# A root-mean-square pooling kernel: the small first piece on partitions 32 to 91 instead of 0 to 29

## The chip, the cores and the metric

One core of one Trainium2 chip, the chip otherwise idle. The metric is the device time of one execution in microseconds (us); lower is better. Beside it stands the *span* of a profiled or timed execution, from the first to the last counted instruction.

## The reference

```python
x = randn(32, 256, 4096) float32;  p = 2.0;  kernel_size = 4
for i in range(4096 // 4):
    window = abs(x[:, :, 4*i:4*i+4]) ** p
    result[:, :, i] = mean(window, axis=-1) ** (1.0 / p)
```

Each output is the root of the mean of four squares. 134.22 MB go in and 33.55 MB go out.

## The kernel before

The input is taken as one flat array. 22 big loads, most of them 128 rows of 13,184 columns (52,736 bytes a row), rotate through three input buffers. ScalarE (ACT) squares a load in place, VectorE (DVE) sums groups of four into an output buffer, ACT takes the root, and a store sends two loads' worth of results out. Loads are issued from the SP queue, the first seven big stores from the ACT queue, the last four from the SP queue.

The total does not divide evenly into such loads. 840 columns times 128 elements, 430 KB (420.0 KB in the views, which count in units of 1024), remain. This *small piece* is loaded first of all, into a corner of an output buffer that is still free:

```python
    Q = 30
    odd = ODD * P // Q                       # 840 * 128 / 30 = 3584
    t = o_tiles[1][0:Q, 0:odd]
    nc.sync.dma_start(out=t, in_=xf[(total - ODD) * P:total * P].rearrange("(p w) -> p w", p=Q))
    ahead = 0
    while ahead < n and loads[ahead][0] < X_SLOTS:
        load(ahead)                          # the first three big loads, same queue
        ahead += 1
    nc.vector.tensor_tensor(out=t, in0=t, in1=t, op=mybir.AluOpType.mult)
    ...                                      # sum of four, root, store of 30 x 896
```

and a big store is issued as soon as its root is taken:

```python
    def root(g, o, ends):
        r = nc.scalar.activation(out=o, in_=o, func=Act.Sqrt, scale=1.0 / k)
        ...
        if ends and g not in late:
            store(g, nc.scalar)
```

Of the kernel before, what the change touches and what calls it, by code (L numbers as in the profile page):

```python
# [1 line left out]

# [4 lines left out]


@with_exitstack
def kernel(  # L10
    ctx: ExitStack,
    tc: tile.TileContext,
    x: bass.AP,
    p: float,
    kernel_size: int,
    out: bass.AP,
):








    nc = tc.nc

    assert float(p) == 2.0, "kernel specialized for p == 2"
    k = int(kernel_size)
    assert k == 4, "kernel specialized for kernel_size == 4"  # L30

    P = nc.NUM_PARTITIONS
    fp32 = mybir.dt.float32
    Act = mybir.ActivationFunctionType
    xf = x.rearrange("b c l -> (b c l)")
    of = out.rearrange("b c l -> (b c l)")
    total = xf.shape[0] // P

    W, O_W = 13184, 6592
    X_SLOTS, O_SLOTS = 3, 2  # L40
    slots = [[(W, [W])]] * 17 + [[(W, [6592, 6592])]]
    slots += [[(6592, [6592]), (6592, [6592])], [(6592, [6592]), (4216, [2112, 2104])]]
    ODD = 840
    groups = [2] * 9 + [3, 1]
    late = {7, 8, 9, 10}
    in_x = {9: (2, 0), 10: (2, 4944)}
    FINE, ENDS, LAG = {21}, {19, 20}, 1
    PAIRS = 15


    loads = [(s, sum(w for w, _ in slot[:j]), *slot[j]) for s, slot in enumerate(slots)
             for j in range(len(slot))]
    n = len(loads)
    assert sum(w for _, _, w, _ in loads) + ODD == total

    firsts = [sum(groups[:g]) for g in range(len(groups))]
    assert sum(groups) == n
    group_of = [g for g, count in enumerate(groups) for _ in range(count)]
    columns = [sum(w for _, _, w, _ in loads[firsts[g]:firsts[g] + groups[g]])
               for g in range(len(groups))]  # L60

    x_pool = ctx.enter_context(tc.tile_pool(name="x_pool", bufs=1))
    o_pool = ctx.enter_context(tc.tile_pool(name="o_pool", bufs=1))

    x_tiles = [x_pool.tile([P, W], fp32, name=f"xt{j}") for j in range(X_SLOTS)]
    o_tiles = [o_pool.tile([P, O_W], fp32, name=f"ot{j}") for j in range(O_SLOTS)]
    ctx.enter_context(tc.manual_schedule())

    def block(flat, g, div):
        at, width = sum(columns[:g]) * P // div, columns[g] * P // div  # L70
        return flat[at:at + width].rearrange("(p w) -> p w", p=P)

    xs = {}
    by_load = []

    def load(i):
        s, at, w, _ = loads[i]
        v = x_tiles[s % X_SLOTS][:, at:at + w]
        g = group_of[i]
        src = sum(loads[j][2] for j in range(firsts[g], i))  # L80
        nc.sync.dma_start(out=v, in_=block(xf, g, 1)[:, src:src + w])  # L81
        xs[i] = v

    ots = {}




    stores = {}
    by_act = []  # L90
    sums = []

    def follows(ins, before):
        for b in before:
            tc.declare_no_dep(ins.ins, b.ins, reason="follows from other waits")

    def store(g, queue):
        stores[g] = queue.dma_start(out=block(of, g, k), in_=ots[g])  # L98

    def root(g, o, ends):  # L100
        r = nc.scalar.activation(out=o, in_=o, func=Act.Sqrt, scale=1.0 / k)  # L101
        follows(r, by_act[:-1] + list(stores.values()))
        by_act.append(r)
        if ends and g not in late:
            store(g, nc.scalar)

    def total_sum(o, v, i):
        add = mybir.AluOpType.add
        if i < PAIRS:
            r = nc.vector.tensor_reduce(  # L110
                out=o, in_=v.rearrange("p (n j) -> p n j", j=k),
                axis=mybir.AxisListType.X, op=add,
            )
            follows(r, sums[:-1])
            sums.append(r)
            return

        q = v.rearrange("p (n j) -> p n j", j=k)
        front = v[:, 0:v.shape[1] // 2]
        h = front.rearrange("p (n j) -> p n j", j=2)  # L120
        r = nc.vector.tensor_tensor(out=h, in0=q[:, :, 0:2], in1=q[:, :, 2:4], op=add)  # L121
        follows(r, sums[:-1] + by_load)
        r = nc.vector.tensor_tensor(out=o, in0=h[:, :, 0], in1=h[:, :, 1], op=add)  # L123
        follows(r, sums[:-1])
        sums.append(r)


    Q = 30
    odd = ODD * P // Q
    t = o_tiles[1][0:Q, 0:odd]  # L130
    nc.sync.dma_start(out=t, in_=xf[(total - ODD) * P:total * P].rearrange("(p w) -> p w", p=Q))  # L131
    ahead = 0
    while ahead < n and loads[ahead][0] < X_SLOTS:
        load(ahead)
        ahead += 1
    nc.vector.tensor_tensor(out=t, in0=t, in1=t, op=mybir.AluOpType.mult)  # L136
    o = o_tiles[1][0:Q, odd:odd + odd // k]
    nc.vector.tensor_reduce(  # L138
        out=o, in_=t.rearrange("p (n j) -> p n j", j=k),
        axis=mybir.AxisListType.X, op=mybir.AluOpType.add,  # L140
    )
    nc.scalar.activation(out=o, in_=o, func=Act.Sqrt, scale=1.0 / k)  # L142
    stores["odd"] = nc.scalar.dma_start(
        out=of[(total - ODD) * P // k:total * P // k].rearrange("(p w) -> p w", p=Q), in_=o,
    )
    pending = []
    done = 0
    for i in range(n):
        s, _, w, chunks = loads[i]
        while ahead < n and loads[ahead][0] < s + X_SLOTS:  # L150
            load(ahead)
            ahead += 1
        g = group_of[i]
        if i == firsts[g]:
            t, first = (o_tiles[g % O_SLOTS], 0) if g not in in_x else (x_tiles[in_x[g][0]], in_x[g][1])
            ots[g] = t[:, first:first + columns[g] // k]
            summed = rooted = 0
        assert sum(chunks) == w
        c = 0
        for step in chunks:  # L160
            v = xs[i][:, c:c + step]
            r = nc.scalar.activation(out=v, in_=v, func=Act.Square)  # L162
            follows(r, by_act[:-1])
            by_act.append(r)
            total_sum(ots[g][:, summed:summed + step // k], v, i)
            while pending and pending[0][0] <= done - LAG:
                root(*pending.pop(0)[1:])
            done += 1
            c += step
            summed += step // k  # L170
            ends = summed == columns[g] // k
            if ends or i in FINE or (i in ENDS and c == w):
                pending.append((done - 1, g, ots[g][:, rooted:summed], ends))
                rooted = summed
    for job in pending:
        root(*job[1:])
    for g in sorted(late):
        store(g, nc.sync)


# [1 line left out]
_INS = ['x', 'p', 'kernel_size']  # L182
_OUTS = [((32, 256, 1024), 'float32')]

_NUMBERS = {'p': 2.0, 'kernel_size': 4}


# [26 lines left out]
```

## Time and profile before

| | before |
|---|---|
| time, median of the first 3 runs | 394.47 us (394.25 to 395.67) |
| span of the profiled run | 392.4 us |
| DVE busy, ACT busy | 68%, 71% |
| share of the 16 DMA engines' time that the two queues take | 99.3% |
| small piece: issue to landing | 4.3 us |
| first big square starts at | 20.66 us |

How to read it: compute engines have time to spare and the DMA engines have none, so look at what those do and at what they do *not* do in each stretch. A transfer is split over the DMA engines: in the records, 16 completion writes follow each big load and 15 the small one. From 24 to 340 us exactly 16 packets are under way for 97% of the time, and 99% of them start within 4 ns of the end of another. I read this as each engine working through its own row of packets one after the other, so a packet that takes longer than its bytes warrant is lost time for that engine. I call this the **loss**: the sum of (time of a packet minus the usual time of its size) over all packets of a stretch, divided by 16.

### The profile page before, as it was taken

What the parts mean: (1) busy time and instruction counts of PE and PEld (TensorE: products, weight loads), DVE (VectorE), ACT (ScalarE), POOL (GpSimd) and SP (SyncE); (2) the same over time, 40 slices, a digit from 0 to 9 for tenths busy, and PEclk for the clock granted to TensorE, in tenths of its full rate; (3) what the DMA queues carried; (4) which work ended last, traced back from release to release, by engine and by line L of the source; (5) the groups of instructions that cost most, each with busy time, mean ns of one, the idle gap of its engine ahead of it and who ended that gap; (6) DMA issues with size and microseconds to landing.
All of it is one profiled execution on the core that took longest, in us unless ns stands there. A gap on an engine that the chain in (4) does not pass through costs nothing.

```text
span 392.4 us, 183 instructions
## 1 busy us (share of the span) xinstructions
DVE 268.5 (68%) x35; ACT 280.2 (71%) x39; POOL 0.2 (0%) x4
## 2 busy tenths in 40 slices
DVE  4307898885769476948693769396928690989481
ACT  1085879919990899099909990998099919999991
POOL 0000000000000000000000000000000000000000
DMA  8999999999999998999999999999999999999997
GB/s 318 425 441 430 446 441 441 411 435 470 430 398 430 473 430 387 430 473 430 411 441 438 430 473 425 392 430 430 430 435 452 446 430 446 409 430 416 446 430 321
DMA packets 4842, 167.77 MB, mean 428 GB/s; under 512 B 558, under 2 KB 558, under 8 KB 716
## 3 DMA queue, kind: packets, MB, share of 16 engines
q1 hardware_dynamic: 3789, 144.04, 85.3%
q10 hardware_dynamic: 1053, 23.73, 14.0%
HBM read 134.22 MB, written 33.55 MB: 428 GB/s over the span
## 4 chain that ended last, share of the span: by engine, by line
DMA 47%; ACT 34%; DVE 16%; SPq 0%; ACTq 0%; issue 0%
DMA xt<-in_x_dram 47%; ACT xt L162 28%; DVE ot L110 14%; ACT ot L101 6%; DVE xt L121 1%; DVE xt L123 1%; ACT xt L101 1%; ACTq L98 0%; SPq L81 0%; SPq L131 0%
## 5 line engine op out<-in xcount | busy, mean ns | idle before, releaser
L162 ACT ACTIVATE xt<-xt 128x13184 f32<-128x13184 f32 (+3 forms) x24 | 222.2, 9272 | 91.4 <-DMA xt<-in_x_dram 89.8
L110 DVE TENSOR_REDUCE ot<-xt 128x3296 f32<-128x13184 f32 x15 | 208.3, 13886 | 88.6 <-ACT xt L162 88.6
L101 ACT ACTIVATE ot<-ot 128x6592 f32<-128x6592 f32 x9 | 51.1, 5681 | 0.0
L121 DVE TENSOR_TENSOR xt<-xt 128x3296 f32<-128x3296 f32 (+3 forms) x9 | 34.5, 3836 | 22.5 <-ACT xt L162 22.2
L123 DVE TENSOR_TENSOR ot<-xt 128x3296 f32<-128x3296 f32 (+1 forms) x4 | 10.9, 2734 | 0.1
L142 ACT ACTIVATE ot<-ot 30x896 f32<-30x896 f32 x1 | 0.9, 948 | 10.9 <-DVE ot L138 10.9
L101 ACT ACTIVATE xt<-xt 128x3296 f32<-128x3296 f32 (+3 forms) x4 | 5.8, 1449 | 2.3 <-DVE xt L123 2.3
L136 DVE TENSOR_TENSOR ot<-ot 30x3584 f32<-30x3584 f32 x1 | 3.9, 3879 | 5.1 <-DMA ot<-in_x_dram 5.1
L123 DVE TENSOR_TENSOR xt<-xt 128x1648 f32<-128x1648 f32 (+2 forms) x5 | 7.0, 1407 | 0.2
L138 DVE TENSOR_REDUCE ot<-ot 30x896 f32<-30x3584 f32 x1 | 3.9, 3874 | 0.0
L142 ACT ACT_TABLE_LOAD x1 | 1.3, 1283 | 0.7 <-PEq L195 0.7
L195 POOL MEMSET const-bfloat16-1.0<- 128x1 bf16 x1 | 0.1, 101 | 0.0
L195 POOL MEMSET const-uint8-127<- 128x1 uint8 x1 | 0.1, 101 | 0.0
L195 POOL MEMSET const-float32-0.0<- 128x1 f32 x1 | 0.1, 98 | 0.2 <-issue 0.2
L195 POOL MEMSET const-float32-1.0<- 128x1 f32 x1 | 0.1, 98 | 0.0
## 6 DMA issues: line engine op xcount, KB each, us to landing
xt<-in_x_dram SPq DMA_DIRECT2D x18, 6592.0 KB, 31.3
out_dram<-ot ACTq DMA_DIRECT2D x7, 3296.0 KB, 27.0
xt<-in_x_dram SPq DMA_DIRECT2D x3, 3296.0 KB, 24.2
out_dram<-ot SPq DMA_DIRECT2D x2, 3296.0 KB, 26.2
out_dram<-xt SPq DMA_DIRECT2D x1, 2472.0 KB, 9.2
xt<-in_x_dram SPq DMA_DIRECT2D x1, 2108.0 KB, 23.7
out_dram<-xt SPq DMA_DIRECT2D x1, 527.0 KB, 5.9
ot<-in_x_dram SPq DMA_DIRECT2D x1, 420.0 KB, 4.3
```

Source lines behind the costliest of these rows:

```text
L101: r = nc.scalar.activation(out=o, in_=o, func=Act.Sqrt, scale=1.0 / k)
L110: r = nc.vector.tensor_reduce(out=o, in_=v.rearrange("p (n j) -> p n j", j=k), axis=mybir.AxisListType.X, op=add,)
L121: r = nc.vector.tensor_tensor(out=h, in0=q[:, :, 0:2], in1=q[:, :, 2:4], op=add)
L123: r = nc.vector.tensor_tensor(out=o, in0=h[:, :, 0], in1=h[:, :, 1], op=add)
L136: nc.vector.tensor_tensor(out=t, in0=t, in1=t, op=mybir.AluOpType.mult)
L138: nc.vector.tensor_reduce(out=o, in_=t.rearrange("p (n j) -> p n j", j=k), axis=mybir.AxisListType.X, op=mybir.AluOpType.add,)
L142: nc.scalar.activation(out=o, in_=o, func=Act.Sqrt, scale=1.0 / k)
L162: r = nc.scalar.activation(out=v, in_=v, func=Act.Square)
L195: nc = _bacc.Bacc("TRN2", target_bir_lowering=False, num_devices=1)
```

## The change

The intent: with 30 rows on partitions 0 to 29, two to each of 15 DMA engines (30 packets, 15 completion writes), the second packets take 741 to 1092 ns where their bytes are worth 529. With 60 half rows on partitions 32 to 91, four to each of the 15 engines, I expected each packet to take the time of its bytes alone, about 265 ns. The arithmetic is split at partition 64 into two sets of instructions.

```diff
-    Q = 30
+    LOW, Q = 32, 60
     odd = ODD * P // Q
-    t = o_tiles[1][0:Q, 0:odd]
-    nc.sync.dma_start(out=t, in_=xf[(total - ODD) * P:total * P].rearrange("(p w) -> p w", p=Q))
+    wide = o_tiles[1]
+    nc.sync.dma_start(
+        out=wide[LOW:LOW + Q, 0:odd],
+        in_=xf[(total - ODD) * P:total * P].rearrange("(p w) -> p w", p=Q),
+    )
 ...
-    nc.vector.tensor_tensor(out=t, in0=t, in1=t, op=mybir.AluOpType.mult)
-    o = o_tiles[1][0:Q, odd:odd + odd // k]
-    nc.vector.tensor_reduce(...)
-    nc.scalar.activation(out=o, in_=o, func=Act.Sqrt, scale=1.0 / k)
+    for a, b in ((LOW, 64), (64, LOW + Q)):
+        t, o = wide[a:b, 0:odd], wide[a:b, odd:odd + odd // k]
+        nc.vector.tensor_tensor(out=t, in0=t, in1=t, op=mybir.AluOpType.mult)
+        nc.vector.tensor_reduce(...)
+        nc.scalar.activation(out=o, in_=o, func=Act.Sqrt, scale=1.0 / k)
 ...                     # the small store takes its rows from the same partitions
```

More of the change, by code (lines that the diff above doesn't have):

```diff
@@ L135 @@
         ahead += 1
-    nc.vector.tensor_tensor(out=t, in0=t, in1=t, op=mybir.AluOpType.mult)
-    o = o_tiles[1][0:Q, odd:odd + odd // k]
-    nc.vector.tensor_reduce(
-        out=o, in_=t.rearrange("p (n j) -> p n j", j=k),
-        axis=mybir.AxisListType.X, op=mybir.AluOpType.add,
-    )
-    nc.scalar.activation(out=o, in_=o, func=Act.Sqrt, scale=1.0 / k)
+    for a, b in ((LOW, 64), (64, LOW + Q)):
+        t, o = wide[a:b, 0:odd], wide[a:b, odd:odd + odd // k]
+        nc.vector.tensor_tensor(out=t, in0=t, in1=t, op=mybir.AluOpType.mult)
+        nc.vector.tensor_reduce(
+            out=o, in_=t.rearrange("p (n j) -> p n j", j=k),
+            axis=mybir.AxisListType.X, op=mybir.AluOpType.add,
+        )
+        nc.scalar.activation(out=o, in_=o, func=Act.Sqrt, scale=1.0 / k)
     stores["odd"] = nc.scalar.dma_start(
-        out=of[(total - ODD) * P // k:total * P // k].rearrange("(p w) -> p w", p=Q), in_=o,
+        out=of[(total - ODD) * P // k:total * P // k].rearrange("(p w) -> p w", p=Q),
+        in_=wide[LOW:LOW + Q, odd:odd + odd // k],
     )
```

## The prediction

> **What bounds the kernel now.** I read the page first (shares of the engines, the DMA row, the queues), then the busy time by stages, then the timeline of the start, and last the single packet records of the trace.
>
> From the page:
>
> ```profile
> span 392.4 us, 183 instructions
> ...
> DVE 268.5 (68%) x35; ACT 280.2 (71%) x39; POOL 0.2 (0%) x4
> ...
> DMA  8999999999999998999999999999999999999997
> ...
> q1 hardware_dynamic: 3789, 144.04, 85.3%
> q10 hardware_dynamic: 1053, 23.73, 14.0%
> HBM read 134.22 MB, written 33.55 MB: 428 GB/s over the span
> ```
>
> The two compute engines idle for about 30% each. The 16 DMA engines are busy in every one of the 40 slices, and the two queues together take 85.3 + 14.0 = 99.3% of them. The stages (us, then DVE, ACT, POOL busy, PE clock, DMA share, GB/s) say the same:
>
> ```profile
> 0.00:8.00 8.00, 2.90 (x1) 1.28 (x1) 0.20 (x4) 1.00 0.89 324
> ...
> 24.00:80.00 56.00, 41.66 (x3) 46.81 (x5) 0.00 (x0) 1.00 1.00 430
> 80.00:340.00 260.00, 183.30 (x15) 184.75 (x21) 0.00 (x0) 1.00 1.00 432
> 340.00:384.00 44.00, 34.82 (x15) 42.46 (x11) 0.00 (x0) 1.00 1.00 432
> ```
>
> From 24 to 384 us the DMA share is 1.00. Only the first 8 us and the tail are below. The kernel is bound by transfers from end to end. The chain that ended last names ACT and DVE for half of the span, but that is only the route by which buffers come free: the queue behind them never ran dry.
>
> A budget: a 52,736-byte packet, half of a 13,184-column row, takes 1947 ns in the median, 27.09 GB/s for one engine, 433.4 GB/s for 16. 167.77 MB at that rate are 387.1 us. The first packet starts at 1.74 us and the last ends at 390.99. So only 390.99 - 1.74 - 387.1 = 2.15 us of engine time is lost in the whole kernel. That is all that any rearrangement of transfers could win.
>
> The start, from the timeline:
>
> ```profile
> 0.73 0.45 SPq L131 DMA_DIRECT2D ot<-in_x_dram  x1
> 1.24 1.30 SPq L81 DMA_DIRECT2D xt<-in_x_dram  x3
> 5.09 3.88 DVE L136 TENSOR_TENSOR ot<-ot 30x3584 f32<-30x3584 f32 x1 [5.09 <-DMA ot<-in_x_dram]
> 9.01 3.87 DVE L138 TENSOR_REDUCE ot<-ot 30x896 f32<-30x3584 f32 x1
> 12.92 0.95 ACT L142 ACTIVATE ot<-ot 30x896 f32<-30x896 f32 x1 [10.90 <-DVE ot L138]
> 13.89 0.64 ACTq L143 DMA_DIRECT2D out_dram<-ot  x1
> 20.66 11.19 ACT L162 ACTIVATE xt<-xt 128x13184 f32<-128x13184 f32 x1 [6.79 <-DMA xt<-in_x_dram]
> ```
>
> The small piece is the first transfer in the queue; the big loads stand right behind it. Its own arithmetic (5.09 to 13.87 us) is over nearly 7 us before the first big load lands at 20.66, so nothing waits for that. Its transfer, however, stands in front of all others on the engines.
>
> The packet records (us from the span's start) of it and of the first big load:
>
> ```
> 14,336-byte packets: 30; first of each engine starts 1.73 to 2.21, takes 542 to 965 ns
>                          second of each engine takes 741 to 1092 ns; last ends 3.98
> first 52,736-byte packets: 16; start 3.03 to 3.98, take 2245 to 2908 ns, end 5.52 to 6.25
> all later ones: 1947 ns median
> last completion write of each engine: 390.32 to 391.00
> ```
>
> At 27.09 GB/s a packet of 14,336 bytes should take 529 ns; the last ones of the small piece take 1085, twice that.
>
> [...]
>
> **The change part by part.**
>
> Bytes: none added. Still 28,672 per engine for 15 engines.
>
> The load. [...] A 3584-byte packet takes 140 ns where its bytes are worth 132, so a packet costs about 8 ns besides, and two more per engine 0.02 us. [...]
>
> What the engines lost before: the 30 packets took 25.34 us together where 30 x 529 ns are 15.89, so 9.45; the 16 first big packets took 39.18 where 16 x 1.949 are 31.18, so 8.00. (9.45 + 8.00) / 16 = 1.09 us per engine. [...] The earliest of the first big packets, starting at 3.03 ahead of any completion write, belongs to the engine that has no share of the small piece[...]; it still took 2473 ns, 0.53 too many. The very last, which began when the small piece was done, had 0.30 too many. I therefore take 0.3 to 0.5 us as start-up of a first big transfer that stays.
>
> The slowest engine sets the end, and its lag is never made up: 391.00 - 6.25 = 384.75 for the latest and 390.32 - 5.52 = 384.80 for the earliest, if lags keep their order. So the quantity to predict is when the slowest engine ends its first big packet, now 6.25. After: start at the latest 2.2, plus 1.08 for four packets, plus some 0.2 for the first packet's latency (my choice), makes 3.5; plus 1.95 + 0.1 to 0.5 for the first big packet makes 5.5 to 6.0. Saved 0.25 to 0.75; with no start-up loss at all, 1.0. I choose **0.65 us**.
>
> Compute. DVE: (3879 - 146) ns are 3584 columns at one per 1.04 ns, so a half instruction is about 1.87 + 0.15 = 2.02 us, four of them 8.1 instead of 7.75. ACT: 13,184 columns take 11.19 us, 0.849 ns each, so 896 columns are 0.76 and the rest of 948 ns is 0.19; two of 448 columns are 2 x 0.57 = 1.14. In all half a microsecond more, off the path: done near 13.5 us, against 20 for the first load. The order of instructions shows two more on DVE, one on ACT, and nothing else moved. Path cost: 0.
>
> The store. 30 packets of 3584 bytes at 140 ns become 60 of 1792 at some 74: per engine 0.28 to 0.30 us, +0.02. It alternates with 1.95 us packets of the loads, so with four per engine it lands some 4 us later; nobody waits for it.
>
> Sum: -0.65 + 0.02 + 0 = about -0.6; 394.47 becomes **393.8 us**, 0.2% less.
>
> **Rivals.**
> (a) The full microsecond: [...]the big packets begin at 3.0 everywhere. For it: the doubled second packets. Against: the free engine's 2473 ns. Time 393.4.
> (b) Nothing: [...] The first packets spread over 0.48 us for 15 engines, 32 ns per engine; if that is per descriptor, 16 ns each, 30 more cost 0.48 us and the start moves from 3.0 to 3.5 on the last engine, which eats most of the gain. Time 394.2 to 394.5. Against: 3.5 is still earlier than 3.98.
> (c) The gain is absorbed: the lag of the slowest engine is not what ends the kernel but the last stores behind ACT. Against: from 340 to 384 us the share is 1.00, so data were still queued when ACT was done. Time 394.4.
> (d) Slower: twice as many, half as long rows in the small store disturb the first loads. At 74 ns each I see at most 0.1 us.
>
> **Range and chances.** (a) and (b) bracket the change at -1.1 and 0. The three runs of before spread from 394.25 to 395.67, so the median itself moves by some tenths. Range 393.1 to 394.7. A 2% change would be 7.9 us, over three times all the engine time lost in the kernel[...]: faster 0.01, within 2% 0.98, slower 0.01.
>
> **What would show it.** Right: the small piece's packets take about 265 ns each, none above 400 after the first of each engine; its load lands about 0.5 us earlier than 4.3 us after issue; the first multiply starts near 4.5 rather than 5.09; the first big square at about 20.0 rather than 20.66; the span is 0.4 to 1.0 shorter with the DMA share still 1.00 in the middle. Wrong: packets of 530 ns for 7168 bytes[...], first big packets starting later than 3.5 (descriptors, rival b), or an earlier first square with an unchanged end (rival c).

Some passages are cut; the cuts are marked. In the paragraph on the load, the terms 2.12 us before and 1.06 after are cut; with the 0.02 for two more packets per engine, which stays, they came to about 1.04 us saved. The sum of -0.65, +0.02 and 0 is about -0.6 us, hence 393.8. Its 0.65 is an estimate from the time at which the slowest engine's first big row ends; that the 60 packets would take the time of their bytes at the measured 27.09 GB/s was my assumption. So was, in rival (b), that 60 rows instead of 30 delay the rows behind them; a *descriptor*, there and in the expectation of e5, stands for one row of a transfer.

## More of the kernel before

All runs quoted here are in the fast state, with a granted clock of 1.00.

Below, *light start* stands for a small piece on partitions 32 to 91, 32 to 95 or 0 to 127, *heavy start* for one on 0 to 29, 0 to 31, 0 to 59, 0 to 63 or 64 to 95.

## The result, and the profile after

The changed kernel took 395.12 us in the median (394.91 to 396.56, 6 runs). The kernel before, taken up to 6 runs on the same chip, stood at 395.54 (394.25 to 395.85). The ratio of the fast runs is 1.0005, with a 95% interval of 0.9983 to 1.0026: no difference. Ratios here are the mean time of one kernel's fast runs over that of the other's fast runs of the same rounds, so they are not quite the ratios of the medians.

The page of the changed kernel answers the page of before line by line:

```profile
span 393.6 us, 186 instructions
...
DVE 268.7 (68%) x37; ACT 280.5 (71%) x40; POOL 0.2 (0%) x4
...
DMA  9999999999999999999999999999999999999997
...
q1 hardware_dynamic: 3819, 144.04, 85.2%
q10 hardware_dynamic: 1083, 23.73, 14.0%
HBM read 134.22 MB, written 33.55 MB: 426 GB/s over the span
```

The bytes are the same, the packets are 60 more. The first digit of the DMA row went from 8 to 9, yet the rate over the span went from 428 to 426. The stages (same columns as in the prediction: us, DVE, ACT, POOL busy, PE clock, DMA share, GB/s) show where:

```profile
0.00:8.00 8.00, 3.88 (x2) 1.28 (x1) 0.20 (x4) 1.00 0.92 370
...
24.00:80.00 56.00, 41.94 (x4) 46.33 (x5) 0.00 (x0) 1.00 1.00 426
80.00:340.00 260.00, 181.94 (x15) 184.00 (x20) 0.00 (x0) 1.00 1.00 432
340.00:384.00 44.00, 34.84 (x14) 42.45 (x12) 0.00 (x0) 1.00 1.00 431
```

The first 8 us move more (370 GB/s, before 324). The stretch from 24 to 80 us moves less (426, before 430), with the engines just as busy: packets there took longer. The start of the timeline:

```profile
0.73 0.45 SPq L132 DMA_DIRECT2D ot<-in_x_dram  x1
1.24 1.30 SPq L81 DMA_DIRECT2D xt<-in_x_dram  x3
4.08 2.02 DVE L142 TENSOR_TENSOR ot<-ot 32x1792 f32<-32x1792 f32 x1 [4.08 <-DMA ot<-in_x_dram]
6.13 2.01 DVE L143 TENSOR_REDUCE ot<-ot 32x448 f32<-32x1792 f32 x1
...
12.27 0.57 ACT L147 ACTIVATE ot<-ot 28x448 f32<-28x448 f32 x1 [3.52 <-DVE ot L143]
12.87 0.64 ACTq L148 DMA_DIRECT2D out_dram<-ot  x1
19.99 11.19 ACT L168 ACTIVATE xt<-xt 128x13184 f32<-128x13184 f32 x1 [7.14 <-DMA xt<-in_x_dram]
```

The small piece is there a microsecond earlier (first multiply at 4.08 instead of 5.09), and the first big square starts at 19.99 instead of 20.66, 0.67 us earlier. So the gain is real. Now the third and the fifth big square, with the first big store between them, in the timeline of before:

```profile
51.77 11.19 ACT L162 ACTIVATE xt<-xt 128x13184 f32<-128x13184 f32 x1 [4.39 <-DMA xt<-in_x_dram]
68.58 0.37 ACTq L98 DMA_DIRECT2D out_dram<-ot  x1
...
88.87 11.19 ACT L162 ACTIVATE xt<-xt 128x13184 f32<-128x13184 f32 x1 [8.68 <-DMA xt<-in_x_dram]
```

and of the changed kernel:

```profile
51.27 11.19 ACT L168 ACTIVATE xt<-xt 128x13184 f32<-128x13184 f32 x1 [4.38 <-DMA xt<-in_x_dram]
68.08 0.37 ACTq L98 DMA_DIRECT2D out_dram<-ot  x1
...
89.25 11.19 ACT L168 ACTIVATE xt<-xt 128x13184 f32<-128x13184 f32 x1 [9.56 <-DMA xt<-in_x_dram]
```

Both squares wait for their load. At the third the changed kernel leads by 0.50 us; at the fifth it trails by 0.38. In between, with the first big store, 0.88 us were lost: 37.10 us from one square to the other before, 37.98 after.

The single packet records, in us from the span's start, say the same for the DMA engines themselves (median and last of the 16 engines' completion writes; loads numbered from 1, and load 18 is the last of full width):

```
                                     before            changed
first big row of an engine ends      5.52 to 6.25      5.18 to 5.67
loss up to 10 us                     1.12              0.51
load 4 complete, median / last       66.68 / 66.91     66.23 / 66.51
loss from 1 us before to 9 us after
  the first big store's issue        0.15              1.11
load 5 complete, median / last       88.17 / 88.49     88.58 / 88.87
load 18 complete, median / last      339.33 / 339.85   340.05 / 341.00
last write of all                    391.00            392.18
```

Two more differences are read off the run lists. The time minus the span is 1.78 us for the kernel before (mean of 44 later runs) and 2.11 to 2.17 for the changed kernel: about **0.36 us lie outside the span**. And the kernel before has times at two levels, near 394.1 and near 395.6: of the 44 later runs, spans lie between 392.2 and 394.2, 24 of them at or above 393.0. I call these the lower and the upper level. The first three runs, from which I predicted, had 394.47, 395.67 and 394.25.

### The profile page after: what moved, and what is told of

Same layout as the page of the kernel before. It is cut to its first block, busy times and chain, and to the rows that moved or that the text cites. A ratio compares the mean times of both kernels' runs of the same rounds, so it can differ in the third digit from the quotient of the medians.

```text
span 393.6 us, 186 instructions
## 1 busy us (share of the span) xinstructions
DVE 268.7 (68%) x37; ACT 280.5 (71%) x40; POOL 0.2 (0%) x4
## 4 chain that ended last, share of the span: by engine, by line
DMA 48%; ACT 34%; DVE 16%; SPq 0%; ACTq 0%; issue 0%
DMA xt<-in_x_dram 48%; ACT xt L168 28%; DVE ot L110 14%; ACT ot L101 6%; DVE xt L121 1%; DVE xt L123 1%; ACT xt L101 1%; ACTq L98 0%; SPq L81 0%; SPq L132 0%
## 5 line engine op out<-in xcount | busy, mean ns | idle before, releaser
L147 ACT ACTIVATE ot<-ot 32x448 f32<-32x448 f32 (+1 forms) x2 | 1.1, 574 | 9.7 <-DVE ot L143 9.7
L142 DVE TENSOR_TENSOR ot<-ot 32x1792 f32<-32x1792 f32 (+1 forms) x2 | 4.0, 2016 | 4.1 <-DMA ot<-in_x_dram 4.1
L143 DVE TENSOR_REDUCE ot<-ot 32x448 f32<-32x1792 f32 (+1 forms) x2 | 4.0, 2010 | 0.1
```

Of the source, the lines that this page charges most:

```text
L143: nc.vector.tensor_reduce(out=o, in_=t.rearrange("p (n j) -> p n j", j=k), axis=mybir.AxisListType.X, op=mybir.AluOpType.add,)
```

## The experiments

Four jobs of four kernels, five rounds each, on the same chip within a job, each timed against the kernel before. All 16 gave correct results. Each loss quoted is read from one profiled execution of its kernel.

### e1: the kernel before again (a control)

No edit.

> The kernel before, unchanged, against itself: a control. Ratio 1.000; the width of its interval is what five rounds can tell. Theory A (the stall of 1.10 us per engine at 70 us in the profile after is chance): this profile too can show stalls of 0.1 to 1 us per engine, at other or the same places, and their sum differs from the 0.28 us per engine that the first profile of before showed beyond the start. Theory B (the change makes that stall, by bringing the engines into step): the excess beyond the start stays near 0.3 us per engine. In both the start loses 1.1 us per engine, the first big packets end at 5.5 to 6.3 us.

Measured: 394.14 us, ratio 0.9994 (0.9975 to 1.0012). Start loss 1.11, loss at the first big store 0.42. One of six runs was at the upper level. So five rounds tell apart about 0.2%, and the loss at the store is not nothing in the kernel before, but under half of the changed kernel's.

### e2: the changed kernel again

No edit.

> The changed kernel again. Both theories: the start as seen, first big packets end at 5.2 to 5.7 us. Theory A: no stall near 1 us per engine at 70 us, or one elsewhere; ratio to before 0.9985 (0.6 us less), from 0.997 to 1.000. Theory B: again a stall of about 1 us per engine at 69 to 75 us, ratio 1.000 to 1.003.

Measured: 395.44 us, ratio 1.0020 (0.9998 to 1.0042). Start loss 0.51, as in the first profile. Loss at the first big store 0.88, again at 69 to 74 us. Chance (theory A) wanted it gone; theory B had it right. Load 4 is complete at 66.17 in the median (e1: 66.57), load 5 at 88.33 (e1: 88.34): a lead of 0.40 us before the store, none after it.

### e3 and e4: three more small loads each

```diff
 # e3: on the kernel before; e4: on the changed kernel, rows LOW:LOW + Q
+    for j in range(3):
+        nc.sync.dma_start(out=x_tiles[2][0:Q, j * odd:(j + 1) * odd], in_=<the small piece>)
```

> The kernel before with the load of the small piece made three times more, into columns of the third input buffer that its first big load overwrites (30 rows on partitions 0 to 29; the copies are read by nobody, the result stays right). Bytes alone: three times 28,672 per engine at 27.09 GB/s, 3.2 us. If [...], three times 2.12 = 6.4 us longer than before, ratio 1.016. If [...]: 3.2 us, ratio 1.008.

> The changed kernel with its small load made three times more, in the same way (60 rows on partitions 32 to 91). Both: four packets of 272 ns per engine and load, three times 1.09 = 3.3 us longer than the changed kernel, ratio to before 1.007. If what is gained at the start reaches the end (the theory of the prediction), this kernel is 3.1 + 0.6 = 3.7 us faster than the one with three more loads of 30 rows; if it is given back on the way, the two differ by under 1 us.

(Conditions of e3: the added loads take twice the time of an engine's bytes, as the doubled packets suggest, or just that time.)

Measured: e3 400.77 us, ratio 1.0156 (1.0135 to 1.0177); e4 398.88 us, ratio 1.0111 (1.0090 to 1.0132), four runs each. Against e1 and e2 of the same rounds, three more loads cost 400.77 - 394.14 = 6.63 us with 30 rows, **2.21 us each**, and 398.88 - 395.44 = 3.44 us with 60 rows on partitions 32 to 91, **1.15 each**. The estimates were 2.12 (twice 28,672 bytes at 27.09 GB/s) and 1.09 (four packets of 272 ns). The medians of e1 and e2 depend on how many runs fell on which level, so these slopes are rough; the engines' median completion of load 4, which comes before that, gives 2.26 ((73.34 - 66.57) / 3) and 1.24 ((69.88 - 66.17) / 3). So a load on partitions 0 to 29 costs nearly twice the time of one on 32 to 91, and this does reach the end of the kernel: it would make about 1.06 us for the one load of the real kernels. But e3 and e4 differ by only 1.89 us, which is neither the 3.7 nor the "under 1 us" of the expectation: beside the part that grows with the number of loads there is a fixed amount that the layout on partitions 32 to 91 pays. With no load added it is 1.30 us slower in these rounds (395.44 - 394.14) though its small load is 1.06 us quicker, so the fixed amount is about 2.4 us here, a part of it the levels.

### e5: 60 rows, but on partitions 0 to 59

```diff
-    LOW, Q = 32, 60
+    LOW, Q = 0, 60
-    for a, b in ((LOW, 64), (64, LOW + Q)):
+    for a, b in ((LOW, LOW + Q),):
```

> The changed kernel with its 60 rows on partitions 0 to 59, arithmetic in one piece again (two DVE instructions, one ACT)[...]. If [...]: second half of the packets near 540 ns for 7168 bytes, start loss 1.0 to 1.1 us per engine, first big packets end at 5.6 to 6.3 us; if the number of descriptors made the difference, the start is like the changed kernel's (0.48 us lost). Time minus span: 1.8 us if the 0.3 us that the changed kernel has outside its span go with its split arithmetic, 2.1 if with the 60 rows.

(Condition: the start's loss goes with the partitions.)

Measured: 395.31 us, ratio 1.0013 (0.9997 to 1.0029). Start loss 1.05, first big rows end at 5.49 to 6.16: as in the kernel before. So it is the partitions, not the finer cut, that make the start heavy or light. Loss at the first big store 0.12. Time minus span 1.74 to 1.83: the extra outside the span is gone with the split arithmetic, although the rows are 60. The time itself is no better than the changed kernel's: five of the six runs are at the upper level, and in the profiled one a single engine ends 1.17 us after the last but one.

### e6: 64 rows on partitions 32 to 95

```diff
-    LOW, Q = 32, 60
+    LOW, Q = 32, 64
```

> The changed kernel with 64 rows on partitions 32 to 95: [...]. Start as in the changed kernel or 0.1 us better[...]. If the stall at the first big store comes from the engines being in step, it is as large as in the changed kernel or larger (0.9 to 1.2 us per engine), and the time 395.0 to 395.6; if it is chance, it can be absent, and the time is then 393.5 to 394.

Measured: 395.49 us, ratio 1.0024 (1.0005 to 1.0042). Start loss 0.52, loss at the first big store 1.09. With 64 rows the loss is as large as with 60 (1.11).

### e7 and e9: the first big store held back

```diff
 # e7 (failed) and e9, before the store:
+        if ends and g == 0:
+            nc.scalar.activation(out=o_tiles[1][:, 3296:6592], in_=o_tiles[0][:, 0:3296], func=Act.Square)   # e7
+            nc.scalar.activation(out=o_tiles[0][:, 0:3296], in_=o_tiles[0][:, 0:3296], func=Act.Copy)        # e9
```

> The changed kernel with one more ACT instruction (some 2.8 us, its result is overwritten) before the first big store is issued, so that this goes out at 71 instead of 68.1 us. If the stall at 70 to 74 us belongs to the issue of that store, it moves by about 3 us, to 73 to 77; if it belongs to what the loads read just then, it stays at 70 us. If only this coincidence of times makes it, it is gone and the time drops to about 393.7.

e7 did not do what I meant. Its store reads nothing that the added instruction writes, so it was issued at 68.18 us beside it. As one more sample of the changed kernel it is of use: 395.56 us, ratio 1.0020 (1.0002 to 1.0039), loss 1.04, same place. In e9 the store must wait:

> The changed kernel with the first big store really held back (the earlier attempt did not: the store did not wait for the added instruction). The added ACT instruction now copies half of that store's data onto itself, 2.9 us, so the store is issued at about 71 us. Theory S (the loss of about 1 us per engine at 70 to 74 us belongs to the store's issue): it moves to 73 to 77 us. Theory L (it belongs to what the loads read at that moment): it stays at 70 to 72.5 us. Theory C (a coincidence of the two): under 0.3 us per engine, and the lowest times go down to 393.8.

Measured: 395.35 us, ratio 1.0005 (0.9985 to 1.0025). Timeline of e9, same columns as above:

```profile
51.26 11.19 ACT L172 ACTIVATE xt<-xt 128x13184 f32<-128x13184 f32 x1 [4.38 <-DMA xt<-in_x_dram]
71.05 0.37 ACTq L98 DMA_DIRECT2D out_dram<-ot  x1
...
87.28 11.19 ACT L172 ACTIVATE xt<-xt 128x13184 f32<-128x13184 f32 x1 [4.63 <-DMA xt<-in_x_dram]
```

The store went out at 71.05, 2.97 us later than in the changed kernel, and the main group of lengthened packets starts at 73.56 to 74.2 us in place of 69.8 to 70.5. The loss is 0.69. (The fifth square comes earlier with fewer store rows in between: 72 had started when load 5 was complete, 100 in the changed kernel.) So **the loss belongs to the store**, not to what the loads read at 70 us. Both e7 and e9 have one ACT instruction more and a time minus span of 1.74 to 1.83 us, like the kernel before.

### e8: the kernel before with the arithmetic in halves

```diff
+    for h in range(2):          # two halves of the columns, 30 partitions each
+        th, oh = ...
         nc.vector.tensor_tensor(...); nc.vector.tensor_reduce(...); nc.scalar.activation(...)
```

> The kernel before with the small piece's arithmetic in two halves of its columns, four DVE and two ACT instructions as in the changed kernel; layout and DMA as before. Theory: compute is off the path, ratio 1.000 inside the span. If the 0.3 us outside the span (time minus span 2.1 in the changed kernel, 1.8 before) goes with the number of instructions, it is 2.1 here; else 1.8.

Measured: 395.25 us, ratio 1.0010 (0.9991 to 1.0030). Start loss 1.12, loss at the store 0.14: nothing changed in the transfers. Time minus span is 2.11 to 2.16 in all six runs. So the split arithmetic (two DVE and one ACT instruction more) is enough to bring the 0.36 us outside the span into the kernel before. It is not what sets them by itself: e7 and e9, with one more ACT instruction, and e12 below, with the big stores in the other queue, have the split arithmetic too and stand at 1.74 to 1.85, while e3, without it, stands at 1.90 to 2.00. What sets the amount is not shown.

### e10: one engine given a lead again (inconclusive)

```diff
 # on the changed kernel, behind the small load
+    nc.sync.dma_start(out=x_tiles[2][LOW:LOW + Q, 0:840], in_=<840 * 60 elements>)
```

> The changed kernel with one more small load (60 rows of 840 columns on partitions 32 to 91, into columns of the third input buffer that its first big load overwrites): 15 engines get four packets of 3360 bytes more, 0.53 us, the sixteenth gets nothing, so that one engine is ahead by about 0.5 us again as in the kernel before[...]. If the loss at the first big store falls on everybody only where no engine is ahead, the 15 lose under 0.3 us and the time is that of the kernel before plus 0 to 0.3 us (outside the span); if the layout makes it in another way, all lose 0.8 us or more and the time is 395.2 to 396.2.

Measured: 396.59 us, ratio 1.0047 (1.0031 to 1.0062). The loss at the store was 0.31, low as the theory wanted. But the start was not what I had built: the engines' first big rows began anywhere between 3.2 and 5.8 us, and the first load was complete at 21.61 in the median instead of 19.25, 2.4 us later for 0.5 us of bytes. The engines' positions were thus stirred up altogether, and the run says nothing about a lead.

### e11 and e15: 32 rows on partitions 0 to 31

```diff
-    Q = 30
+    Q = 32
```

> The kernel before with 32 rows on partitions 0 to 31 instead of 30: [...]. If it is the engine ahead that keeps the others from the loss at the first big store, all 16 now lose about 1 us there and the time is 395.0 to 395.5; if [...], the time is 394.1 to 394.6 as before.

> 32 rows on partitions 0 to 31 again. If its gain of 0.2% was real: median 393.9 to 394.2, no run above 394.6, ratio 0.997 to 0.999. If it was chance: some runs near 395.5, as in the kernel before, ratio near 1.000.

(Condition of e11: the loss goes with partitions from 64 up.)

Measured: e11 394.04 us (393.84 to 394.26), ratio 0.9981 (0.9966 to 0.9995); e15, the same kernel in a later job, 395.17 us (393.89 to 395.61), ratio 0.9987 (0.9968 to 1.0007). Loss at the store 0.16 and 0.18. With 32 rows I meant to leave no engine ahead of the others; if so (how the 32 rows fell to the engines is not shown), my idea that an engine ahead protects the others falls. The gain of e11 is not confirmed: in e15 four of six runs were at the upper level. Timeline of e11:

```profile
51.59 11.19 ACT L162 ACTIVATE xt<-xt 128x13184 f32<-128x13184 f32 x1 [4.39 <-DMA xt<-in_x_dram]
68.40 0.36 ACTq L98 DMA_DIRECT2D out_dram<-ot  x1
...
88.70 11.19 ACT L162 ACTIVATE xt<-xt 128x13184 f32<-128x13184 f32 x1 [8.71 <-DMA xt<-in_x_dram]
```

37.11 us from the third to the fifth square, as in the kernel before.

### e12: the changed kernel with the big stores on the SP queue

```diff
-            store(g, nc.scalar)
+            store(g, nc.sync)
```

> The changed kernel with its seven big stores issued from the SP queue, behind the loads, instead of the ACT queue: reads and writes then follow one another on each engine instead of alternating row by row. Bytes are the same. If alternation at the start of a store costs the 1 us, it is gone at 70 us and the lowest span is 391.9 to 392.2, lower than before's 392.2; if the hand-over from reads to writes costs by itself, the losses appear at other places and the time is 395 or more. Chance that it beats both kernels: 0.35.

Measured: 396.35 us, ratio 1.0045 (1.0027 to 1.0064). Each engine now finishes all eight rows of load 5 before the eight rows of the store. No loss follows the store's issue at 68.29, but the *last* row of load 5, the one ahead of the engine's first store row, takes 0.49 to 1.12 us too long on every engine (rows starting at 79.8 to 80.8; first store rows at 82.6 to 83.2). All lengthened packets between 73.9 and 80.8 us make a loss of 0.98. So it is not the alternation of load and store rows. Most of the loss (0.75 of the 0.98) falls on the row ahead of an engine's first big store row. In the changed kernel, too, 0.74 of the 1.11 us fall on the 16 load rows that start at 69.8 to 70.5 (2.38 to 3.19 us each in place of 1.95), ahead of the first store rows at 72.5 and later, and the rest on load rows behind these. I had given this kernel a chance of 0.35 of beating both kernels; its median is above both. Its time minus span is 1.76 to 1.85.

### e13: 128 rows on all partitions

```diff
-    Q = 30
+    Q = 128
```

> The kernel before with the small piece as 128 rows on all partitions: [...]arithmetic in one piece (time minus span 1.8 us). Start loss 0.5 us per engine or less. If [...], it is 0.7 to 1.1 us per engine at 70 to 74 us, median time 394.6 to 395.6; if it comes from the odd cut of 60 or 64 rows, it is under 0.3 us and the time is 393.4 to 393.8.

(Condition: the loss goes with a light start.)

Measured: 395.47 us, ratio 0.9998 (0.9983 to 1.0014). Start loss 0.56, loss at the first big store 0.64. Timeline of e13:

```profile
51.30 11.19 ACT L162 ACTIVATE xt<-xt 128x13184 f32<-128x13184 f32 x1 [4.38 <-DMA xt<-in_x_dram]
68.10 0.34 ACTq L98 DMA_DIRECT2D out_dram<-ot  x1
...
89.36 11.19 ACT L162 ACTIVATE xt<-xt 128x13184 f32<-128x13184 f32 x1 [9.68 <-DMA xt<-in_x_dram]
```

38.06 us between the squares, as in the changed kernel. A light start, even with the plainest layout and one-piece arithmetic, comes with the loss, though at 0.64 it is a little under the 0.7 that I had allowed for this. With time minus span at 1.75 to 1.83 it still doesn't beat the kernel before.

### e14 and e16: 32 rows on partitions 64 to 95, and 64 rows on partitions 0 to 63

```diff
-    LOW, Q = 32, 60
+    LOW, Q = 64, 32     # e14: partitions 64 to 95
+    LOW, Q = 0, 64      # e16: partitions 0 to 63
-    for a, b in ((LOW, 64), (64, LOW + Q)):
+    for a, b in ((LOW, LOW + Q),):
```

> 32 rows on partitions 64 to 95: [...]. Start loss about 1.1 us per engine[...]. If [...], there is none here (under 0.3 us) and the time is 393.8 to 394.3; if [...], it is 0.7 to 1.1 us and the time is 395 or more.

> 64 rows on partitions 0 to 63: [...]. Start loss about 1.0 us per engine. If [...]: under 0.3 us there, time 393.8 to 394.3 with no run above 394.6. If the cut into 64 rows makes it: 0.7 to 1.1 us.

(Conditions of e14: the loss goes with a light start, or with partitions from 64 up; of e16: a heavy start without an engine ahead keeps the loss and late engines away.)

Measured: e14 394.63 us, ratio 0.9984 (0.9965 to 1.0002), start loss 1.04, loss at the store 0.33; e16 394.31 us, ratio 0.9979 (0.9962 to 0.9996), start loss 1.11, loss at the store 0.11. e14's loss is a little over the 0.3 that I had allowed if a light start is the cause, and far under the 0.7 to 1.1 for the partitions from 64 up. In e16's profiled run one engine was 2 us late from its first row on, which no theory of mine had.

### All profiled runs side by side

| kernel | small piece on partitions | start loss, us | loss at the first big store, us |
|---|---|---|---|
| before, e1, e8 (30 rows) | 0 to 29, heavy | 1.12, 1.11, 1.12 | 0.15, 0.42, 0.14 |
| e5, e16 (60, 64 rows) | 0 to 59, 0 to 63, heavy | 1.05, 1.11 | 0.12, 0.11 |
| e11, e15 (32 rows) | 0 to 31, heavy | 1.10, 1.09 | 0.16, 0.18 |
| e14 (32 rows) | 64 to 95, heavy | 1.04 | 0.33 |
| e3 (four small loads) | 0 to 29, heavy | 4.26 | 0.01 |
| changed, e2, e7 (60 rows) | 32 to 91, light | 0.51, 0.51, 0.53 | 1.11, 0.88, 1.04 |
| e6 (64 rows), e13 (128 rows) | 32 to 95, 0 to 127, light | 0.52, 0.56 | 1.09, 0.64 |
| e9 (store later) | 32 to 91, light | 0.44 | 0.69 |
| e4 (four small loads) | 32 to 91, light | 0.96 | 0.47 |
| e10 (engines stirred up) | 32 to 91, light | 1.13 | 0.31 |

Without e3, e4 and e10, which add transfers, and e12, whose store stands in another queue: eight profiles with a heavy start lose 0.11 to 0.42 us at the first big store, six with a light one 0.64 to 1.11. None of these falls between. The division is not clean: of the profiles left out, e10 and e4, on the partitions of a light start, lost only 0.31 and 0.47.

## Why the prediction was wrong

**What bounds the kernel**: right. The DMA engines are the bound in every version; nothing in compute mattered within the span.

**The shorter small load**: right. On partitions 0 to 29 the last packets take about twice as long as their bytes are worth (1085 ns in place of 529 for 14,336 bytes), on 32 to 91 about as long (272 ns in the median in place of 265 for 7168). The explanation that I gave for this is not shown. e3 and e4 confirm the step as 2.21 against 1.15 us per load, at the end of the kernel. The small load was complete 3.3 us after its issue instead of 4.3: a whole microsecond, where I had expected half of one. Rival (b), later big rows, falls: the first big row of the free engine started at 2.81 us, before at 3.04. One detail was wrong: I wrote that no small packet would take over 400 ns after each engine's first, and six took 524 to 964.

**The size at the start**: right in the first pair of profiles, smaller in the second. I chose 0.65 us. The slowest engine's first big row ended at 5.67 instead of 6.25, 0.58 earlier; the first square started at 19.99, where I had written "about 20.0". In the second pair (e1, e2) that row ended only 0.15 earlier (5.92 instead of 6.07) and the first square started 0.32 earlier (20.17 instead of 20.49), though the median engine gained 0.61 on its first big row. The 0.3 to 0.5 us that I held to be a start-up cost of the first big rows were mostly absent in the first profile, where 14 of the 16 took the plain 1947 to 1959 ns and two took longer (2194 and 2658 ns); in e2 six took 2195 to 2642, so some of it can stay. The start's loss fell from 1.12 to 0.51 in both pairs, since the small packets kept some of it too.

**The step that failed** reads in the prediction: "The slowest engine sets the end, and its lag is never made up". In the one profile that I had, lags did persist from the first row to the last write, and I took this for a law. Its first half held; the second did not: from the slowest engine's first big row to the last write it is 384.75 us in the kernel before, but 386.51 in the changed kernel (392.18 - 5.67), and 384.91 against 385.85 in e1 and e2. What the runs showed in its place: at the first big store the engines of the changed kernel lose 0.9 to 1.1 us, where those of the kernel before lose 0.15 to 0.42. At load 4 the lead was 0.45 us in the median, at load 5 it was a lag of 0.41 (in the second pair of profiles, e1 and e2, a lead of 0.40 and then none). This is what rival (c) said of the outcome, "the gain is absorbed", but not by its mechanism: nobody waited for ACT, the data were slower.

**"Path cost: 0" for the arithmetic** was right inside the span and missed 0.36 us outside it. e8 shows that the split arithmetic is enough for it, without any change of layout; e7, e9 and e12 show that it does not always bring it.

**The store of the small piece**: I said it would land some 4 us later with nobody waiting. Both were so. The lines of the DMA view (issue, KB, us to landing), before:

```profile
ot<-in_x_dram SPq DMA_DIRECT2D x1, 420.0 KB, 4.3
out_dram<-ot ACTq DMA_DIRECT2D x1, 105.0 KB, 8.3
```

and after the change:

```profile
ot<-in_x_dram SPq DMA_DIRECT2D x1, 420.0 KB, 3.3
out_dram<-ot ACTq DMA_DIRECT2D x1, 105.0 KB, 12.6
```

**The range** was too narrow for a further reason. I let the median of before move "by some tenths". It has two levels 1.4 us apart, and the three runs in hand (one of three at 395.67) showed that. In the profiles of e5, e8, e14, e15 and e16, whose spans lie at 393.4 or above, one single engine ends 1.2 to 1.3 us after all others; in e1 and e11 (392.4 and 392.2) none does. So the upper level comes with one late engine. It falls behind at no fixed place: it is over a microsecond behind the next by load 5 in e15, by load 14 in e5 and e14, and only by load 17 in e8. Why is not shown. The kernel before happened to stand at 395.54 in the run that decided, and the changed kernel's 395.12 was outside 393.1 to 394.7 while being 0.42 below that.

A slip besides: the prediction calls a 52,736-byte packet half of a row. It is a whole row, 13,184 columns of 4 bytes. No number depends on it.

**What adds up.** From the first pair of profiles: -0.45 us (median engine, at load 4), then +0.86 at the first big store, then +0.31 up to load 18 (340.05 - 339.33 = 0.72 behind), then +0.46 because the last engine trails further in this profile, makes the +1.18 of the last write; with 0.36 outside the span it is 1.5 us, the 395.73 against 394.21 of the two profiled runs. In the medians of six runs most of this is hidden by the two levels.

**What stays open.** Why a light start is followed by the loss at the first big store is not shown. By 30 us the arithmetic of the small piece is long over, and no other instruction differs. What does differ is how the 16 engines stand to each other within half a microsecond or so; that they carry the effect is argued, not shown, since the records do not name the engine, and the one attempt to set their positions (e10) went wrong. How wide they are spread does not decide it: e4, with first big rows ending between 8.00 and 10.24 us, loses less than the changed kernel, with 5.18 to 5.67.

**No version beats both kernels with certainty.** e11, e14, e15 and e16, with 32 or 64 rows and a heavy start, have ratios of 0.9979 to 0.9987 to the kernel before. The intervals of e11 and e16 end just below 1 (0.9995 and 0.9996), but the repeat of e11 reaches 1.0007, the lowest times (393.84 to 394.14) are those of the kernel before (393.96), and the difference lies in how many runs fell on the upper level.

## What to carry to other kernels

A gain at the start of a transfer-bound kernel has to be followed past the first point where the traffic changes kind: here 0.45 us were in hand at 66 us and gone at 88. When a tile has fewer than 128 rows, try which partitions it is loaded to, since the choice nearly doubled the time here (430 KB took 2.21 us on 0 to 29, 1.15 on 32 to 91); to see such a cost beside the noise, repeat the transfer, as e3 and e4 did, and take the slope. And before predicting a tenth of a percent, look at whether the times of the kernel have one level or two.
